# A two-layer SSD and HGRN2 encoder step: the norms' sums of squares as two fp32r passes, and one norm placed earlier in pieces

## The chip, the cores and the metric

The kernel runs on one core of a Trainium2 chip. The engines are TensorE (PE, with its weight loads as PEld), VectorE (DVE), ScalarE (ACT), GpSimd (POOL) and SyncE (SP, which issues the DMAs). The metric is the device time of one execution in microseconds (us), as a median over runs. [...]

## The reference

A trunk of two layers takes one step for a prompt of 1024 frames and for a running stream of 32 frames, with the same weights and a model width of 1024. Cut to what matters here:

```python
def rmsnorm(x, w):
    y = x * rsqrt(mean(x * x, axis=-1) + 1e-6)
    return y * w

for layer in (0, 1):
    h = rmsnorm(x, norm_w)
    x = x + (ssd_mixer if layer == 0 else hgrn_mixer)(h, ...)
    x = x + swiglu(rmsnorm(x, ffn_norm_w), w_gate, w_up, w_down)
y = rmsnorm(x, final_norm_w)
```

Inside the SSD mixer each of 4 groups of 512 channels is normed by its own mean square, and inside the HGRN mixer each of 8 heads of 128 channels:

```python
yg = yg * rsqrt(mean(yg * yg, axis=-1) + 1e-6)                 # SSD, per group
o  = o  * rsqrt(mean(o * o,  axis=-1) + 1e-6) * gnorm_w        # HGRN, per head
```

The outputs are the two sequences and the recurrent states and convolution rows of both streams.

## The kernel before

**Layout.** Channels lie on the 128 partitions, frames on the free axis. The frames are worked in two halves: the first has 512 frames of the prompt, the second the other 512 and the 32 of the running stream, 544 in all. [...] The residual stream `acc[h][m]` (8 tiles of 128 channels for each half) stays in SBUF.

**Products.** To keep fp32 accuracy with fp32r matmuls, each operand is split into a high part (an ACT copy to fp32r) and a low part (a DVE subtraction, L273 and L274 in `split`), and `product` adds three passes: high by high (L303), high by low (L304), low by high (L305). Weights are split in the same way after each load (L292, L293). The FFNs save multiplications with a Strassen-like scheme (`ffn_unit`, its three passes at L940 to L942).

**Norms.** `rstd_of` squares its tiles on ACT (L312), adds them on DVE into one tile `tot` (L316), and sums over the partitions with one fp32 matmul for each block against a 128x128 tile of ones (L320). ACT then takes Ln with scale and bias (L321) and Exp of -0.5 times that (L322). It is called for 4 SSD gates and 8 HGRN gates in each half, for `x_stat` (the statistics alone, kept in a tile that the caller names), and from `norm`, which goes on to scale and split all 8 tiles in one go (L353, L357, L358). `norm` is wrapped so that the scheduler takes its instructions 600 steps earlier than their place in the program (`HP`, `lifted`). `norm_pieces` (L860) does the scaling and splitting as 8 tasks for each block, without that lift, so that a caller can lay them among other tasks.

**Tiles.** The tag "n" has 4 buffers (`BUFS`), used for the squares, `rstd`, the scaled tile `xf`, the HGRN layer's decay factors, and two evacuation tiles of each FFN unit. The normed and split residual of the first half lies in the fixed tiles `XN`; that of the HGRN layer's second half takes 12 buffers of "x" and 4 of "cb" (`XN2`). In the HGRN layer the recurrent states use `st[0]` and `st[1]`; `st[2]` and `st[3]` are free.

**Order.** The framework's scheduler lays out each engine's instructions when the program is built, by program order, priority and when it expects operands to be ready; on the chip each engine takes its instructions in that order. The HGRN layer runs 16 units, heads 0 to 7 of the first half, then of the second. While the chunks of one head's recurrence run, a list of tasks is dealt out among them: the gate projection of this head, the output product of the last pair of heads (every second head), and the projections f, q and v of the next head. A gate (`hgrn_gate`) with its `rstd_of` ends each head. Before the change, head 6 of the first half has `norm(1, C_HGN, xns[1], XN2)` as its last task (L827); the projections of the second half's head 0, in head 7's list, are the first to read it. The input of that norm, `acc[1]`, is complete before the HGRN layer begins.

Of the kernel before, what the change touches and what calls it, by code (L numbers as in the profile page):

```python
# [9 lines left out]
F32R = mybir.dt.float32r  # L10
U32 = mybir.dt.uint32
AF = mybir.ActivationFunctionType
# [4 lines left out]
P = 128  # L17
# [5 lines left out]
LEN = (H1, SEQ - H1 + NS)  # L23
# [14 lines left out]
C_SSDN, C_CB, C_FFN, C_HGN, C_GN, C_HG, C_LB = 0, 8, 32, 48, 56, 72, 73  # L38
# [10 lines left out]
def trunk_kernel(ctx, tc, x_prompt, x_sample, state_ssd, cache_conv, state_hgrn,  # L49
# [5 lines left out]
    V, A, G, PE = nc.vector, nc.scalar, nc.gpsimd, nc.tensor  # L55

    cp = ctx.enter_context(tc.tile_pool(name="cp", bufs=1))
# [8 lines left out]
    def nm(s):  # L66
        uid[0] += 1
        return f"{s}_{uid[0]}"

    def T(tag, s, dt=F32):  # L70
        return tp.tile([P, WIDTH[tag]], dt, tag=tag, bufs=BUFS[tag], name=nm(s))

    def slot(tag, s):
        return T(tag, s, F32R) if isinstance(tag, str) else tag
# [19 lines left out]
    def psum_sc():  # L94
        return pm.tile([P, 512], F32, tag="sc", bufs=3, name=nm("sc"))

    def act(out, in_, f, **kw):
        A.activation(out=out, in_=in_, func=f, **kw)  # L98
# [32 lines left out]
    def place(w):  # L131
        used[0] += -(-w // 16) * 16
        return fixed[:, used[0] - -(-w // 16) * 16:][:, :w]
# [4 lines left out]
    make_identity(nc, ident)  # L138
    ones = place(P)
    V.memset(ones, 1.0)  # L140
    epsc = place(1)
    V.memset(epsc, EPS)
    lss = place(13)
# [127 lines left out]
    def split(xf, w, pair):  # L271
        xh, xl = pair
        act(xh[:, :w], xf, AF.Copy)  # L273
        tt(xl[:, :w], xf, xh[:, :w].bitcast(F32), SUB)  # L274
        return pair
# [31 lines left out]
    def rstd_of(tiles, blocks, scale, width, keep=None):  # L307

        tot = None
        for i, t in enumerate(tiles):  # L310
            sq = T("n", "sq")
            act(sq[:, :width], t, AF.Square)  # L312
            if tot is None:
                tot = sq
            else:
                tt(tot[:, :width], tot[:, :width], sq[:, :width], ADD)  # L316
        r = keep if keep is not None else T("n", "rstd")
        for (b0, bn) in blocks:
            ps = psum_sc()
            PE.matmul(ps[:, :bn], ones, tot[:, b0:b0 + bn], start=True, stop=True)  # L320
            act(r[:, b0:b0 + bn], ps[:, :bn], AF.Ln, bias=epsc[:, 0:1], scale=scale)  # L321
        act(r[:, :width], r[:, :width], AF.Exp, scale=-0.5)  # L322
        return r
# [3 lines left out]
    XN = [xnt[:, i] for i in range(16)]  # L327
    XN2 = ["x"] * 12 + ["cb"] * 4
# [15 lines left out]
    @lifted("norm")  # L344
    def norm(h, wc, out, tags, blocks=None, r=None):

        for (b0, bn) in blocks or ((0, LEN[h]),):
            mmb = BLK[h] if blocks is None else [(0, bn)]
            if r is None:
                r = rstd_of([acc[h][m][:, b0:b0 + bn] for m in range(KD)], mmb, 1.0 / D, bn)  # L350
            for m in range(KD):
                xf = T("n", "xf")
                stt(xf[:, :bn], acc[h][m][:, b0:b0 + bn], vc[:, wc + m:wc + m + 1], r[:, :bn], MUL, MUL)  # L353
                if m == len(out):
                    out.append((slot(tags[2 * m], "h"), slot(tags[2 * m + 1], "l")))
                xh, xl = out[m]
                act(xh[:, b0:b0 + bn], xf[:, :bn], AF.Copy)  # L357
                tt(xl[:, b0:b0 + bn], xf[:, :bn], xh[:, b0:b0 + bn].bitcast(F32), SUB)  # L358
        return out
# [8 lines left out]
    st = [place(TW) for _ in range(NG)]  # L368
# [442 lines left out]
    def hgrn_layer(after):  # L811
        units = [(h, e) for h in range(2) for e in range(8)]
        us = [{"S": None} for _ in units]
        for f in (hgrn_f, hgrn_q, hgrn_v):
            f(0, 0, us[0])
        for i, (h, e) in enumerate(units):
            u = us[i]
            tasks = [lambda: hgrn_g(h, e, u)]
            if e % 2 == 0 and i:
                ph, pe = units[i - 1]  # L820
                tasks += [lambda m4=m4: hgrn_out(ph, pe // 2, m4, [us[i - 2]["y"], us[i - 1]["y"]])
                          for m4 in range(2)]
            if i + 1 < len(units):
                nh, ne = units[i + 1]
                tasks += [lambda f=f: f(nh, ne, us[i + 1]) for f in (hgrn_f, hgrn_q, hgrn_v)]
            if (h, e) == (0, 6):
                tasks.append(lambda: norm(1, C_HGN, xns[1], XN2))  # L827
            if (h, e) == (1, 6):
                tasks += after[:1]
            if (h, e) == (1, 7):  # L830
                tasks += after[1:]
            u["o"] = T("ys", "ho")
            if e % 2 == 0:
                yt = sp.tile([P, 4 * TW], F32R, tag="Y", bufs=1, name=nm("hy"))[:, :4 * LEN[1]]
                yp = yt.rearrange("p (j t) -> p j t", j=4)
            u["yp"] = yp
            nch = len(CHUNKS[h])
            for c in range(nch):
                second = hgrn_chunk(h, e, c, u)
                q = -(-len(tasks) // (nch - c))  # L840
                for i2, t in enumerate(tasks[:q]):
                    if i2 == HB2:
                        second()
                    t()
                if q <= HB2:
                    second()
                tasks = tasks[q:]
            hgrn_gate(h, e, u)
        return [lambda m4=m4: hgrn_out(1, 3, m4, [us[-2]["y"], us[-1]["y"]]) for m4 in range(2)]
# [6 lines left out]
    def x_stat(h, keep):  # L856

        return rstd_of([acc[h][m][:, :LEN[h]] for m in range(KD)], BLK[h], 1.0 / D, LEN[h], keep)

    def norm_pieces(h, wc, out, blocks, r):  # L860

        def piece(m, b0, bn):
            xf = T("n", "xf")
            stt(xf[:, :bn], acc[h][m][:, b0:b0 + bn], vc[:, wc + m:wc + m + 1], r[:, b0:b0 + bn], MUL, MUL)
            if m == len(out):
                out.append((XN[2 * m], XN[2 * m + 1]))
            xh, xl = out[m]
            act(xh[:, b0:b0 + bn], xf[:, :bn], AF.Copy)
            tt(xl[:, b0:b0 + bn], xf[:, :bn], xh[:, b0:b0 + bn].bitcast(F32), SUB)
        return [lambda m=m, b=b: piece(m, *b) for b in blocks for m in range(KD)]  # L870
# [209 lines left out]
    def mixed(a, b):  # L1080

        out, k = [], 0
        for i, x in enumerate(a):
            out.append(x)
            while k < len(b) and k * len(a) < (i + 1) * len(b):
                out.append(b[k])
                k += 1
        return out + b[k:]
# [98 lines left out]
    xns, dts = [[], []], [None, None]  # L1187
# [12 lines left out]
    due, r = mixer_ffn(lambda after: ssd_layer(after, w0), 0, C_FFN, True)  # L1200
    for s, dst in ((0, conv_p), (1, conv_s)):
        ps = psum_sc()
# [7 lines left out]
    due, r = mixer_ffn(hgrn_layer, 1, C_FFN + 8, False)  # L1210
# [41 lines left out]
```

## Time and profile before

| What | us |
|---|---|
| median of 3 runs | 2893.22 |
| lowest and highest | 2892.77 and 2895.23 |
| the profiled execution's own time | 2895.71 |
| its span in the profile | 2894.0 |
| PE busy | 2843.8 |
| DVE busy | 2158.1 |
| ACT busy | 1563.9 |
| HGRN layer, roughly | 1600 to 2200 of the span |

The profile shows one execution. The time of an execution is that of the span and 1.7 us around it. In a timeline row the first number is the start from the span's start, the second the time covered, then engine, line, operation, tiles (out<-in), shape and how many instructions are merged in the row; in brackets stands how long the engine stood idle before it and what released it. Since L98, L101 and L104 are helpers that record every ACT, DVE tensor and DVE scalar-tensor operation, one reads those by the names of their tiles. The ends of matmuls are modelled, so their pace is read from one start to the next.

### The profile page before, as it was taken

Reading aid. Unit: us, or ns where it says so; the run is one execution under the profiler, and the core shown is the slowest. Engines: PE = TensorE matmul, PEld = TensorE weight load, DVE = VectorE, ACT = ScalarE, POOL = GpSimd, SP = SyncE. Lnnn points to the kernel's source line nnn. Section 1 sums busy time; section 2 is a strip of 40 time slices with the busy share of each in tenths; the row PEclk is TensorE's granted clock in tenths of the full one; section 3 lists DMA queues with packets and bytes.
Section 4 is the critical chain, followed back from the end, with each engine's and each line's share of the span. In section 5 each row is a group of like instructions: output and inputs, shape, how many; then the busy total and the mean of one; then the engine's idle time right before and its main releaser. Section 6 shows DMA issues by size and latency. Waiting matters only on the chain. (4 is left out here: it accounts for less than half of the span.)

```text
span 2894.0 us, 49037 instructions
## 1 busy us (share of the span) xinstructions
PE 2843.8 (98%) x19655; PEld 2615.4 (90%) x19655; DVE 2158.1 (75%) x3787; ACT 1563.9 (54%) x2951; POOL 43.2 (1%) x156
## 2 busy tenths in 40 slices
PE   7999999999999999999999999999999999999998
PEld 6777888999988999999999888899988999999998
DVE  6877797777787877887777555755568877887777
ACT  6755555564643644455444655755564644554445
POOL 0000000000000000000000000000000000000000
PEclk9999999999999999999999999999999999999999
DMA  5443434444332333323333222222222332333223
GB/s 159 121 108 111 107 79 126 113 111 108 106 90 88 106 106 95 110 81 101 97 96 114 79 75 73 60 77 74 79 78 92 113 95 91 118 96 95 88 88 112
DMA packets 401343, 283.39 MB, mean 98 GB/s; under 512 B 28873, under 2 KB 386778, under 8 KB 401114
## 3 DMA queue, kind: packets, MB, share of 16 engines
q1 hardware_dynamic: 401114, 280.25, 33.3%
q8 instruction: 154, 2.52, 0.4%
q14 instruction: 75, 0.61, 0.1%
HBM read 272.39 MB, written 7.82 MB: 97 GB/s over the span
## 5 line engine op out<-in xcount | busy, mean ns | idle before, releaser
L98 ACT ACTIVATE wh<-raw 128x512 fp32r<-128x512 f32 (+1 forms) x688 | 557.1, 818 | 556.8 <-PE mm L304 431.3
L303 PE MATMUL mm<-xn,wh 128*128 128x272 f32 (+2 forms) x1552 | 524.2, 338 | 1.7 <-ACT xn L98 1.3
L304 PE MATMUL mm<-xn,wh 128*128 128x272 f32 (+2 forms) x1552 | 519.0, 335 | 1.2 <-DVE xn L101 1.2
L305 PE MATMUL mm<-xn,wl 128*128 128x272 f32 (+2 forms) x1552 | 518.0, 334 | 1.2 <-DVE wl L101 1.2
L101 DVE TENSOR_TENSOR wl<-raw,wh 128x1024 fp32r<-128x1024 f32 x308 | 375.5, 1221 | 75.4 <-ACT wh L98 57.4
L101 DVE TENSOR_TENSOR fixed<-mm,fixed 128x272 f32<-128x272 f32 (+1 forms) x512 | 262.5, 523 | 194.4 <-PE mm L305 192.8
L304 PE MATMUL mm<-fl,wh 128*128 128x272 f32 (+1 forms) x1056 | 342.3, 324 | 0.9 <-DVE fl L101 0.8
L303 PE MATMUL mm<-fh,wh 128*128 128x272 f32 (+1 forms) x1056 | 341.4, 325 | 0.6 <-DVE fixed L101 0.6
L305 PE MATMUL mm<-fh,wl 128*128 128x272 f32 (+1 forms) x1056 | 341.7, 324 | 0.0
L303 PEld LDWEIGHTS mm<-xn,wh 128*128 128x128 f32 x1552 | 292.9, 189 | 32.1 <-issue 2.8
L305 PEld LDWEIGHTS mm<-xn,wl 128*128 128x128 f32 x1552 | 292.9, 189 | 31.1 <-issue 2.0
L304 PEld LDWEIGHTS mm<-xn,wh 128*128 128x128 f32 x1552 | 292.5, 188 | 29.3 <-DVE xn L101 1.7
L101 DVE TENSOR_TENSOR wh<-raw,wh 128x512 fp32r<-128x512 f32 x380 | 256.8, 686 | 43.5 <-ACT wh L98 40.9
L940 PE MATMUL mm<-th,wh 128*128 128x272 f32 (+1 forms) x912 | 260.2, 285 | 0.1
L942 PE MATMUL mm<-th,wh 128*128 128x272 f32 (+1 forms) x912 | 259.6, 285 | 0.2 <-DVE wh L101 0.2
L941 PE MATMUL mm<-tl,wh 128*128 128x272 f32 (+1 forms) x912 | 259.6, 285 | 0.0
L304 PEld LDWEIGHTS mm<-fl,wh 128*128 128x128 f32 x1056 | 198.7, 188 | 17.2 <-DVE fl L101 2.4
L303 PEld LDWEIGHTS mm<-fh,wh 128*128 128x128 f32 x1056 | 198.3, 188 | 16.6 <-DVE fixed L101 1.0
L305 PEld LDWEIGHTS mm<-fh,wl 128*128 128x128 f32 x1056 | 198.6, 188 | 15.3
L940 PEld LDWEIGHTS mm<-th,wh 128*128 128x128 f32 x912 | 171.6, 188 | 2.0 <-ACT s L98 1.4
L941 PE MATMUL sc<-xn,wh 128*128 128x272 f32 (+1 forms) x608 | 173.1, 285 | 0.0
L942 PE MATMUL sc<-xn,wh 128*128 128x272 f32 (+1 forms) x608 | 172.8, 284 | 0.0
(247 smaller groups left out, 6628.9 us busy)
## 6 DMA issues: line engine op xcount, KB each, us to landing
raw<-in_ffn_w_down_dram SPq DMA_DIRECT2D x90, 512.0 KB, 3.5
raw<-in_ffn_w_gate_dram SPq DMA_DIRECT2D x88, 512.0 KB, 3.9
raw<-in_ffn_w_up_dram SPq DMA_DIRECT2D x88, 512.0 KB, 4.8
raw<-in_ssd_in_w_dram SPq DMA_DIRECT2D x80, 512.0 KB, 4.2
raw<-in_hgrn_in_w_dram SPq DMA_DIRECT2D x64, 512.0 KB, 4.3
cumB<-cumd SPq DMA_DIRECT2D x64, 256.0 KB, 5.0
raw<-in_ssd_out_w_dram SPq DMA_DIRECT2D x32, 512.0 KB, 3.6
raw<-in_hgrn_out_w_dram SPq DMA_DIRECT2D x16, 512.0 KB, 3.3
```

Source lines behind the costliest of these rows:

```text
L98: A.activation(out=out, in_=in_, func=f, **kw)
L101: (eng or V).tensor_tensor(out=out, in0=a, in1=b, op=op)
L303: PE.matmul(ps[:, :bn], a, mh, start=(k == 0), stop=False)
L304: PE.matmul(ps[:, :bn], a, ml, start=False, stop=False)
L305: PE.matmul(ps[:, :bn], b, mh, start=False, stop=(k == n - 1))
L940: PE.matmul(ps[:, :n], a, mh, start=(k == 0 and not more), stop=False, skip_group_check=True)
L941: PE.matmul(ps[:, :n], a, ml, start=False, stop=False, skip_group_check=True)
L942: PE.matmul(ps[:, :n], b, mh, start=False, stop=(k == 3), skip_group_check=True)
```

## The change

There are two parts. First, `rstd_of` splits `tot` into a high and a low fp32r tile (`th`, `tl`, both of tag "n") and adds two fp32r passes against an fp32r copy of the ones in PSUM, where one fp32 matmul stood. Second, in the HGRN layer the second half's norm is taken apart: the statistics become the last task of head 5 (`x_stat`, kept in `st[2]`), and the scaling and splitting become eight pieces (one block of all 544 frames) laid evenly among head 6's tasks. `norm_pieces` gets an argument for the tiles it writes.

```diff
     ones = place(P)
     V.memset(ones, 1.0)
+    onesr = cp.tile([P, P], F32R, name="onesr")
+    A.activation(out=onesr, in_=ones, func=AF.Copy)
...
         r = keep if keep is not None else T("n", "rstd")
+        th, tl = split(tot[:, :width], width, (T("n", "th", F32R), T("n", "tl", F32R)))
         for (b0, bn) in blocks:
             ps = psum_sc()
-            PE.matmul(ps[:, :bn], ones, tot[:, b0:b0 + bn], start=True, stop=True)
+            PE.matmul(ps[:, :bn], onesr, th[:, b0:b0 + bn], start=True, stop=False)
+            PE.matmul(ps[:, :bn], onesr, tl[:, b0:b0 + bn], start=False, stop=True)
             act(r[:, b0:b0 + bn], ps[:, :bn], AF.Ln, bias=epsc[:, 0:1], scale=scale)
...
     def hgrn_layer(after):
         units = [(h, e) for h in range(2) for e in range(8)]
         us = [{"S": None} for _ in units]
+        r = []
...
+            if (h, e) == (0, 5):
+                tasks.append(lambda: r.append(x_stat(1, st[2])))
             if (h, e) == (0, 6):
-                tasks.append(lambda: norm(1, C_HGN, xns[1], XN2))
+                tasks = mixed(tasks, norm_pieces(1, C_HGN, xns[1], ((0, LEN[1]),), r[0], XN2))
...
-    def norm_pieces(h, wc, out, blocks, r):
+    def norm_pieces(h, wc, out, blocks, r, tags=XN):
...
             if m == len(out):
-                out.append((XN[2 * m], XN[2 * m + 1]))
+                out.append((slot(tags[2 * m], "h"), slot(tags[2 * m + 1], "l")))
```

`mixed` (L1080) lays the second list evenly among the first, so head 6's list becomes: gate projection, two pieces, output product, a piece, output product, a piece, f, two pieces, q, a piece, v, a piece.

## The prediction

> **What bounds the kernel now.** I read the page first, then the waits of PE, then windows around the largest wait, then the timeline there, and last the groups of instructions for the price of one.
>
> ```profile
> span 2894.0 us, 49037 instructions
> PE 2843.8 (98%) x19655; PEld 2615.4 (90%) x19655; DVE 2158.1 (75%) x3787; ACT 1563.9 (54%) x2951; POOL 43.2 (1%) x156
> ```
>
> PE is busy 98% of the span, but a matmul's end is modelled, so the pace has to come from starts. The timeline gives it (first and last row of a run of equal matmuls, and a sum of squares with the instruction behind it):
>
> ```profile
> 1898.03 0.29 PE L303 MATMUL mm<-h,wh 128*128 128x272 f32 x1
> ...
> 1900.91 0.28 PE L305 MATMUL mm<-h,wl 128*128 128x272 f32 x1
> ...
> 1817.78 0.39 PE L303 MATMUL mm<-xn,wh 128*128 128x512 f32 x1
> ...
> 1825.87 0.40 PE L305 MATMUL mm<-xn,wl 128*128 128x512 f32 x1
> ...
> 1903.76 1.08 PE L320 MATMUL sc<-sq,fixed 128*128 128x272 f32 x4
> 1904.68 0.38 PE L757 MATMUL sc<-hq,hk 128*128 128x128 f32 x2
> ...
> 1785.69 1.02 PE L320 MATMUL sc<-sq,fixed 128*128 128x512 f32 x2
> 1786.55 0.38 PE L757 MATMUL sc<-hq,hk 128*128 128x128 f32 x2
> ```
>
> The first pair is 24 matmuls, so 23 steps in 2.88 us: 0.125 us for an fp32r pass over 272 columns. The second is 36, 35 steps in 8.09 us: 0.231 us for 512 columns. They start without a pause, so PE is the bound by pace too. The plain fp32 product of L320 shows as two records for each block. In a second half (two blocks, x4) it holds PE for 1904.68 - 1903.76 = 0.92 us; in a first half (one block, x2) for 1786.55 - 1785.69 = 0.86 us.
>
> The waits of PE, and the windows of the one that matters here:
>
> ```profile
> PE mm L303 <- ACT h L98: 3.2, 1, 3.2
> PE sc L320 <- DVE sq L101: 2.7, 3, 1.7
> ```
> ```profile
> 960.00:985.00 25.00, 23.27 (x147) 20.79 (x147) 21.48 (x37) 16.36 (x30) 0.00 (x0) 1.00 0.24 79
> 1600.00:1826.00 226.00, 226.00 (x1097) 185.19 (x1095) 127.09 (x234) 129.90 (x204) 0.00 (x0) 1.00 0.26 73
> 1829.80:1833.00 3.20, 0.05 (x2) 0.02 (x1) 1.55 (x3) 2.82 (x5) 0.00 (x0) 1.00 0.21 79
> 1833.00:1834.80 1.80, 1.11 (x5) 0.72 (x5) 1.80 (x4) 1.80 (x3) 0.00 (x0) 1.00 0.00 0
> 1834.80:1838.30 3.50, 3.38 (x15) 3.38 (x16) 3.50 (x6) 0.83 (x2) 0.00 (x0) 0.51 0.33 94
> 1838.30:1842.00 3.70, 3.70 (x31) 3.70 (x31) 3.70 (x7) 1.96 (x4) 0.00 (x0) 1.00 0.14 53
> 1842.00:2130.00 288.00, 287.44 (x2216) 278.25 (x2215) 168.39 (x378) 167.19 (x295) 0.00 (x0) 1.00 0.27 76
> ```
>
> Columns are length, then busy time and count of PE, PEld, DVE, ACT, POOL, then granted clock, DMA share and GB/s. At 1829.8 PE stands still for 3.2 us, limps for 1.8 us, and then runs 3.5 us at a granted clock of 0.51: 15 matmuls, where the next window has 31 in 3.70 us. [...]
>
> The chain behind that pause, from the timeline:
>
> ```profile
> 1826.59 1.18 PE L320 MATMUL sc<-sq,fixed 128*128 128x272 f32 x4 [0.32 <-DVE sq L101]
> ...
> 1829.47 1.28 ACT L98 ACT_TABLE_LOAD   x1
> 1830.76 0.66 ACT L98 ACTIVATE rstd<-rstd 128x544 f32<-128x544 f32 x1
> ...
> 1831.45 2.18 DVE L104 SCALAR_TENSOR_TENSOR xf<-fixed,rstd 128x544 f32<-128x544 f32 x3 [2.81 <-ACT rstd L98]
> ...
> 1832.27 0.66 ACT L98 ACTIVATE h<-xf 128x544 fp32r<-128x544 f32 x1 [0.37 <-DVE xf L104]
> ...
> 1832.98 0.76 PE L303 MATMUL mm<-h,wh 128*128 128x272 f32 x4 [3.15 <-ACT h L98]
> ```
>
> This is the HGRN layer's norm of the second half: sums, Ln, Exp, scale and split in a row, with the first second-half projection waiting at the end.
>
> **The change part by part.** *1. The fp32 passes.*
>
> ```profile
> L320 PE MATMUL sc<-sq,fixed x90: 390/393/697, 133.6 to 2270.4; 128*128 128x272 f32 x60, 128*128 128x512 f32 x30
> ```
>
> The code calls `rstd_of` 15 times in each half (4 SSD gates, 8 HGRN gates, 3 norms or statistics): 15 x 2 records of 512 and 15 x 2 blocks x 2 records of 272, which is this row. The new product is two fp32r passes for each block, the same kind as L303. First half: 0.86 - 2 x 0.231 = 0.40 us, times 15 is 6.0. Second half: 0.92 - 4 x 0.125 = 0.42 us, times 15 is 6.3. Together **-12.3 us** of PE. [...]
>
> *2. The split in front of it.* Every call gains one ACT copy to fp32r and one DVE subtraction. The same two on a tile of the same size:
>
> ```profile
> L98 ACT ACTIVATE th<-xt 128x544 fp32r<-128x544 f32 x16 | 10.4, 653 | 11.4 <-DVE xt L101 11.2
> L101 DVE TENSOR_TENSOR tl<-xt,th 128x544 fp32r<-128x544 f32 x16 | 11.5, 720 | 0.1
> ```
>
> That is 0.65 and 0.72 us, 30 times: 20 us on ACT (54% busy) and 22 us on DVE (75%), hidden as load; what can cost is the 1.37 us of latency. What waits behind it is queued on PE, which takes matmuls in the planned order, and on ACT, where the Ln stands behind the copy. A typical HGRN gate, and the consumer of its result:
>
> ```profile
> 1934.09 0.66 ACT L98 ACTIVATE sq<-ho 128x544 f32<-128x544 f32 x1
> 1934.77 1.28 ACT L98 ACT_TABLE_LOAD   x1
> 1934.80 1.18 PE L320 MATMUL sc<-sq,fixed 128*128 128x272 f32 x4
> 1936.06 0.49 ACT L98 ACTIVATE rstd<-sc,fixed 128x272 f32<-128x272 f32 x1
> ...
> 1942.80 0.65 PE L303 MATMUL mm<-hy,wh 128*128 128x272 f32 x3
> 1943.09 0.72 DVE L101 TENSOR_TENSOR hy<-ho,hy 128x544 fp32r<-128x544 f32 x1
> ...
> 1944.41 0.29 PE L304 MATMUL mm<-hy,wh 128*128 128x272 f32 x1
> ```
>
> The table load for Ln already takes 1.28 us between Square and Ln. With the split it starts one copy later and covers the subtraction and the shorter passes, so Ln moves by about 0.65 us, not 1.37. An even head's result is wanted only with the next head's; an odd head's is read the moment it is there (1942.80). Five accumulators let PE do 15 matmuls (1.9 us) of the even head's share first, so of the 0.65 us I charge 0.3 us in each of the three pairs of the second half: **+1.0 us**. In the first half the same 15 matmuls are 3.5 us long and cover it. Bounds: 0, and 7 pairs at the full 1.37 us, 9.6 us. SSD gates have the next group's six convolutions between them and their consumer; cost nothing, and 1.37 us each if that cover were gone (then up to 11 us for eight).
>
> *3. Two statistics inside the FFNs*, where DVE is full (21.48 of 25 us in the window 960:985 above) and PE already stands at L320:
>
> ```profile
> 974.92 1.19 PE L320 MATMUL sc<-sq,fixed 128*128 128x272 f32 x4 [1.73 <-DVE sq L101]
> ...
> 2269.57 1.18 PE L320 MATMUL sc<-sq,fixed 128*128 128x272 f32 x4 [0.61 <-DVE sq L101]
> ```
>
> The split can add up to 1.37 us to each (+2.7), or the plan moves the product behind other matmuls and the wait itself goes (-2.3). I take 0.5 us each, **+1.0 us**. Four buffers of "n" hold the two evacuation tiles of a unit, the total, and now `th` and `tl`; `tl` may have to wait until the unit in flight has freed one, which is why I don't take zero.
>
> *4. The HGRN norm a head sooner.* Statistics go to the end of head 5's tasks, scaling and splitting become eight pieces among head 6's, and the first reader is head 7's task list. A head of the first half lasts some 27 us, from the sums of head 4's gate
>
> ```profile
> 1758.15 1.12 PE L320 MATMUL sc<-sq,fixed 128*128 128x512 f32 x2
> ```
>
> to those of head 5 at 1785.69; the chain takes 6.4 us (1826.59 to 1832.98). Its ACT and DVE work is the same as before and only moves; no DMA moves. So the pause goes with its slow clock: from 1829.8 to 1838.3 PE started 2 + 5 + 15 = 22 matmuls in 8.5 us, at 0.125 us each 2.75 us of work: **-5.7 us**. Late next are the weights of that projection, which were there already (the wait names `h` alone). Bounds: 0 and -5.7, with the 0.3 us at 1826.59 besides.
>
> *5.* The fp32r copy of `ones` is one 128-wide copy while the first loads are under way: nothing, at most the 0.65 us of the wider copy.
>
> Sum: -12.3 + 1.0 + 1.0 - 5.7 = -16.0 us. The profiled execution took 2895.71 us (span 2894.0), so it would take 2879.7; against the median of 2893.22, 2.5 us below it, **2877 us**.
>
> **The rivals.**
> *A, a wait takes the pause's place.* The statistics of the moved norm use "n" buffers just ahead of head 5's gate. Eight squares and seven sums in a row:
>
> ```profile
> L98 ACT ACTIVATE sq<-fixed 128x544 f32<-128x544 f32 x24 | 14.5, 650 | 0.0
> L101 DVE TENSOR_TENSOR sq<-sq,sq 128x544 f32<-128x544 f32 x33 | 23.8, 721 | 4.4 <-ACT sq L98 3.8
> ```
>
> 8 x 0.65 + 7 x 0.72 = 10.2 us; if the gate's buffers come only after them, the pair's output product is late by that less the 3.5 us of cover, 6.7 us, and the pause is paid back: 2893.2 - 12.3 + 2.0 - 5.7 + 6.7 = 2884. For it: gate and statistics share four buffers. Against: their input is finished long before, and DVE is 56% busy there (127.09 of 226).
> *B, PE isn't the bound.* [...] As a mechanism of this kernel: if a tenth of PE's time were slack, shorter passes would end in waits and only the pause would go: 2893.2 - 5.7 = 2887.5. Against: weight loads fill 278.25 of 288 us with 272 columns and 185.19 of 226 with 512, which is a load of 0.19 us against 0.231 us of matmul; the share follows the width, not slack. The same time, 2887 to 2890, comes out if the fp32r passes cost what L320 costs now, so that the change didn't do what it says.
> *C, slower.* PE takes its queue in order. If every sum of squares stood at its old place in that order, PE would wait for copy and subtraction, 1.37 us, at each of 30 calls: +41.1 - 12.3 - 5.7 = +23, 2916 us. It decides from 0.6 us a call on, (12.3 + 5.7) / 30. Against: today 30 calls stand 2.7 us for DVE in three waits, though the total is ready just ahead of many of them, so the order is laid out by when operands are due, and the split is laid out with it.
> *D, dearer latencies.* The waits of parts 2 and 3 near their upper bounds, +12.3 instead of +2: 2887.5.
>
> **How the numbers follow.** Forecast (2872 to 2881): 0.61. A: 0.13. D, shading up to 2887: 0.13. B or its like: 0.07. C: 0.06. The low end is -12.3 - 5.7 - 2.3 - 0.3 = -20.6, 2872; the high end takes in A and D up to their far ends, 2888. A measurement of this kernel can tell about 0.2%, 5.8 us, from no change: faster, below 2887.4, is the forecast, A and most of D, 0.86; within, 0.08; slower, C, 0.06.
>
> **What would show it.** Right: the L320 records become 0.125 and 0.231 us apart; no wait of L303 for `h` near 1830 and no window there at a clock of 0.51; copy and subtraction at 0.65 and 0.72 us, 30 each; the waits at the sum of squares stay within a few us in all. Wrong: a wait of PE for `tl` at many calls (C), a wait for `hy` after head 5 (A) or in each second-half pair (D), or PE's total lower by 12 us with the span unmoved (B).

## The result, and the profile after

| | before | after |
|---|---|---|
| median, us | 2893.47 (16 runs, 2890.63 to 2895.23) | 2900.14 (16 runs, 2897.48 to 2904.92) |
| ratio of after to before | | 1.0024, 95% interval 1.0016 to 1.0031 |
| profiled execution, us | 2895.71 | 2902.1 |
| its span, us | 2894.0 | 2900.4 |

The kernel became 0.24% slower; the forecast was 2877 us, 0.57% faster. Here is the head of the page of after:

```profile
span 2900.4 us, 49056 instructions
PE 2840.5 (98%) x19655; PEld 2616.5 (90%) x19655; DVE 2174.8 (75%) x3817; ACT 1578.5 (54%) x2982; POOL 58.5 (2%) x156
```

PE is busy 3.3 us less than before while the span is 6.4 us longer: the shorter passes are there, and PE stands still more. The waits of PE in after (engine, line, what was waited for: us in all, times, longest):

```profile
PE mm L307 <- DVE wl L101: 7.2, 4, 4.1
...
PE sc L776 <- ACT hkv L98: 3.8, 3, 1.9
PE mm L305 <- ACT xn L98: 3.7, 5, 2.1
...
PE sc L323 <- ACT th L98: 3.2, 4, 1.4
...
PE mm L305 <- ACT pre L98: 2.6, 1, 2.6
...
PE mm L306 <- DVE hy L101: 1.4, 2, 0.7
```

The 3.2 us for `h` that the prediction quoted is no longer in the list. In its place stand waits for the low part of weights (`wl`), for a tile of the normed residual (`xn`), a projection's evacuation (`pre`) and a chunk's state (`hkv`). Only the row for `th` names a tile that the change made. (Lines are four higher than before; L305 to L307 are the three passes of `product`, L323 and L324 the two passes of the sum, L776 was L772.)

Both traces have 19655 matmuls, so one can follow where the time went by subtracting the start of the n-th matmul before from the start of the n-th after. This table is worked out so from both traces:

| stretch of before, us | after falls behind by, us | what is there |
|---|---|---|
| 0 to 417 | -2.7 | start-up and passes |
| 417 to 470 | +3.3 | a 4.06 us wait for `wl`, then half clock |
| 470 to 740 | -0.8 | passes |
| 740 to 760 | +4.4 | waits for `wl` and `pre` |
| 760 to 1770 | -3.5 | passes; a half-clock stretch of before is missing |
| 1770 to 1820 | +7.9 | head 5's gate is late, then half clock |
| 1820 to 1860 | -6.4 | the pause of before is gone |
| 1860 to 2125 | -1.4 | passes, less what the pairs of heads lose |
| 2125 to 2160 | +3.7 | a wait for `xn`, then half clock |
| 2160 to the end | +1.9 | mostly a half-clock stretch at 2547 |

The sum is +6.4 us, the difference of the spans. The windows of after show the clock in these places (length, then busy time and count of PE, PEld, DVE, ACT, POOL, granted clock, DMA share, GB/s):

```profile
422.00:426.27 4.27, 0.21 (x2) 0.00 (x0) 4.15 (x10) 3.39 (x7) 0.74 (x2) 1.00 0.24 37
427.30:430.70 3.40, 3.40 (x17) 3.40 (x17) 3.33 (x5) 1.55 (x2) 0.35 (x1) 0.50 1.08 325
1799.50:1809.70 10.20, 8.66 (x24) 6.67 (x25) 6.50 (x12) 3.56 (x8) 0.00 (x0) 0.50 0.24 67
1829.00:1834.80 5.80, 5.80 (x27) 4.72 (x26) 5.15 (x9) 4.59 (x9) 0.00 (x0) 1.00 0.00 0
2137.40:2140.80 3.40, 3.40 (x10) 2.69 (x9) 3.40 (x6) 2.15 (x4) 0.00 (x0) 0.50 0.00 0
2547.00:2550.40 3.40, 3.40 (x17) 3.40 (x17) 3.26 (x6) 0.92 (x2) 0.00 (x0) 0.50 0.00 0
```

Where before paused (1829 to 1834.8), PE of after works without a break at full clock. But between 64 and 2870 us it runs 3.4 + 10.2 + 3.4 + 3.4 = 20.4 us at half clock; before had 6.8 (3.4 at 1834.8 and 3.4 at 1247.7). In such a stretch passes of 272 columns start 0.227 us apart (13 steps from 2547.09 to 2550.04), where 0.125 us is their step at full clock, so at most half of the 13.6 us more, 6.8 us, is time lost in this one execution. Each of the four starts in a wait of PE or within 1.7 us of the end of one (4.06, 1.94, 2.09 and 1.26 us long); that the wait brings it about is not shown. Three places have to be read closer.

**The wait at 422 us, in the SSD layer.** The timeline of after (start, duration, engine, line, operation, tiles; in brackets the idle time before it and its releaser):

```profile
420.87 1.27 DVE L401 TENSOR_TENSOR_SCAN dt<-fixed,dt 128x544 f32<-128x544 f32 x1
...
422.18 0.65 ACT L98 ACTIVATE dt<-dt 32x544 f32<-32x544 f32 x1 [5.16 <-DVE dt L401]
...
423.32 0.79 DVE L101 TENSOR_TENSOR dt<-dt 32x512 f32<-32x512 f32 x2
...
424.39 0.69 DVE L101 TENSOR_TENSOR yl<-Y,yh 128x512 fp32r<-128x512 f32 x1
...
425.00 1.22 DVE L101 TENSOR_TENSOR wl<-raw,wh 128x1024 fp32r<-128x1024 f32 x1
...
426.27 0.39 PE L307 MATMUL mm<-xn,wl 128*128 128x272 f32 x1 [4.06 <-DVE wl L101]
```

and the same three operations before:

```profile
423.37 1.27 DVE L397 TENSOR_TENSOR_SCAN dt<-fixed,dt 128x544 f32<-128x544 f32 x1
...
424.57 1.19 DVE L101 TENSOR_TENSOR wl<-raw,wh 128x1024 fp32r<-128x1024 f32 x1
...
425.82 0.40 PE L305 MATMUL mm<-xn,wl 128*128 128x272 f32 x1 [0.83 <-DVE wl L101]
```

Before, DVE made `wl` right behind the scan. In after it stands behind the rest of the `dt` chain and a `yl`, and ACT stands 5.16 us for the scan, with its other work behind the operation on `dt` that waits. DVE is not slower (1.22 us against 1.19); its order is another. No `th` and no `tl` is in these rows.

**The output product of a pair of heads.** After, second half, first pair:

```profile
1935.59 0.66 ACT L98 ACTIVATE sq<-ho 128x544 f32<-128x544 f32 x1
...
1936.28 0.66 ACT L98 ACTIVATE th<-sq 128x544 fp32r<-128x544 f32 x1
...
1938.25 0.49 ACT L98 ACTIVATE rstd<-sc,fixed 128x272 f32<-128x272 f32 x1
...
1941.00 0.65 ACT L98 ACTIVATE rstd<-rstd 128x544 f32<-128x544 f32 x1
...
1942.36 0.29 DVE L101 TENSOR_TENSOR fixed<-fixed,sc 128x128 f32<-128x128 f32 x1 [4.29 <-PE sc L776]
...
1942.53 0.37 PE L305 MATMUL mm<-hy,wh 128*128 128x272 f32 x1
...
1942.91 0.78 DVE L104 SCALAR_TENSOR_TENSOR ho<-ho,fixed,rstd 128x544 f32<-128x544 f32 x1
...
1944.71 0.66 ACT L98 ACTIVATE hy<-ho 128x544 fp32r<-128x544 f32 x1 [0.40 <-DVE ho L101]
...
1944.99 1.22 DVE L101 TENSOR_TENSOR wl<-raw,wh 128x1024 fp32r<-128x1024 f32 x1
...
1946.12 0.72 DVE L101 TENSOR_TENSOR hy<-ho,hy 128x544 fp32r<-128x544 f32 x1
```

and before, besides the rows that the prediction shows:

```profile
1939.45 0.65 ACT L98 ACTIVATE rstd<-rstd 128x544 f32<-128x544 f32 x1
...
1940.14 0.78 DVE L104 SCALAR_TENSOR_TENSOR ho<-ho,fixed,rstd 128x544 f32<-128x544 f32 x1
...
1941.94 1.23 DVE L101 TENSOR_TENSOR wl<-raw,wh 128x1024 fp32r<-128x1024 f32 x1
```

From Square to Ln it takes 1938.25 - 1935.59 = 2.66 us; before it took 1936.06 - 1934.09 = 1.97 (the prediction's rows): 0.69 us more, where 0.65 was expected. By the Exp this is made up: 1941.00 - 1935.59 = 5.41 us after Square, 1939.45 - 1934.09 = 5.36 before. But from Square to the low part of `hy` it takes 1946.12 - 1935.59 = 10.53 us against 1943.09 - 1934.09 = 9.00: 1.53 us more. The low part follows a `wl` in both. What is new is ahead of the scaling: before, DVE scales `ho` right behind the Exp (1940.14); after, it stands 4.29 us at an update of the recurrent state, which waits for PE and is laid out ahead of the scaling, and scales at 1942.91, though the Exp has ended at 1941.65. So here too it is DVE's order, and not the split's latency.

PE starts the product 1942.53 - 1935.59 = 6.94 us after Square, 7.28 before, and runs out of passes that do without the low part. From the first to the last start of its 96 passes it takes 14.25, 14.33 and 14.02 us in the three second-half pairs, 12.66, 12.64 and 12.66 before. Not all of that is lost: PE does 14 matmuls of the chunks in between, 4 before, and stands idle for at most 0.37 us. What is lost shows from one pair's first start to the next one's: 74.25 and 74.44 us in the second half, 74.64 and 74.67 before. Two heads should have saved 0.84 us there by their shorter passes, so a pair loses 0.4 to 0.6 us.

The first two pairs of the first half take 12.21 us, 11.32 before, with no other matmul more and 0.68 us idle; from start to start it is 66.06 us, 65.96 before, where 0.80 less was due. This loss of 0.9 us is not the split's, as `e3_passes_only` will show.

**Head 5's gate.** The moved statistics and the gate, in after:

```profile
1787.62 0.66 ACT L98 ACTIVATE th<-sq 128x544 fp32r<-128x544 f32 x1 [1.04 <-DVE sq L101]
...
1792.84 0.61 ACT L98 ACTIVATE sq<-ho 128x512 f32<-128x512 f32 x1
...
1796.38 0.48 PE L307 MATMUL mm<-hy,wl 128*128 128x512 f32 x1
...
1800.30 0.79 PE L776 MATMUL sc<-hkv 128*128 128x128 f32 x2 [1.94 <-ACT hkv L98]
...
1804.64 0.69 DVE L101 TENSOR_TENSOR hy<-ho,hy 128x512 fp32r<-128x512 f32 x1
```

The statistics' copy waits on ACT for their last sum, their Ln and Exp follow, and head 5's Square starts only at 1792.84; the low part of its `hy` is made at 1804.64. PE began that output product at 1791.0 and had used up what it could do of it at 1796.38; the next pass of it starts at 1804.53. That is the place that rival A named. Between the Ln of the statistics at 1789.93 and the Square ACT has no idle time: it is ACT's queue that is full there, and no row shows a wait for a buffer.

### The profile page after: what moved, and what is told of

Same layout as the page of the kernel before. It is cut to its first block, busy times and chain, and to the rows that moved or that the text cites. A ratio compares the mean times of both kernels' runs of the same rounds, so it can differ in the third digit from the quotient of the medians.

```text
span 2900.4 us, 49056 instructions
## 1 busy us (share of the span) xinstructions
PE 2840.5 (98%) x19655; PEld 2616.5 (90%) x19655; DVE 2174.8 (75%) x3817; ACT 1578.5 (54%) x2982; POOL 58.5 (2%) x156
## 4 chain that ended last, share of the span: by engine, by line
PE 86%; DVE 7%; ACT 3%; DMA 2%; issue 1%; SPq 0%; POOL 0%; DVEq 0%; ACTq 0%; POOLq 0%
PE mm L305 18%; PE mm L307 18%; PE mm L306 18%; PE mm L949 5%; PE mm L947 5%; PE mm L948 5%; PE sc L949 3%; PE sc L947 3%; PE sc L948 3%; PE sc L548 1%; PE sc L537 1%; DVE fixed L101 1%; PE sc L534 1%; DVE wh L101 1%; DMA fixed<-in_ssd_D_dram 1%
## 5 line engine op out<-in xcount | busy, mean ns | idle before, releaser
L305 PE MATMUL mm<-xn,wh 128*128 128x272 f32 (+2 forms) x1552 | 523.5, 338 | 6.8 <-ACT xn L98 3.7
L307 PE MATMUL mm<-xn,wl 128*128 128x272 f32 (+2 forms) x1552 | 518.7, 335 | 5.8 <-DVE wl L101 5.8
L305 PE MATMUL mm<-fh,wh 128*128 128x272 f32 (+1 forms) x1056 | 341.4, 325 | 0.6 <-DVE fixed L101 0.6
L307 PE MATMUL mm<-fh,wl 128*128 128x272 f32 (+1 forms) x1056 | 341.4, 324 | 0.0
L305 PEld LDWEIGHTS mm<-xn,wh 128*128 128x128 f32 x1552 | 293.4, 189 | 36.7 <-ACT xn L98 4.8
L307 PEld LDWEIGHTS mm<-xn,wl 128*128 128x128 f32 x1552 | 293.7, 189 | 35.9 <-DVE wl L101 6.7
L305 PEld LDWEIGHTS mm<-fh,wh 128*128 128x128 f32 x1056 | 198.4, 188 | 16.6 <-DVE fixed L101 1.0
L307 PEld LDWEIGHTS mm<-fh,wl 128*128 128x128 f32 x1056 | 198.7, 188 | 15.2
```

The costliest lines, as they stand in the source:

```text
L305: PE.matmul(ps[:, :bn], a, mh, start=(k == 0), stop=False)
L307: PE.matmul(ps[:, :bn], b, mh, start=False, stop=(k == n - 1))
```

## The experiments

Three explanations stood against each other at first: the split's latency in front of the sum; the place of its copy in ACT's queue, with what stands behind it; and the new norm's statistics ahead of head 5's gate. A fourth came out of the runs: two more instructions in the queues, and shorter passes, change the order that the scheduler lays out.

### The two parts alone, and the passes without the split

`e1_split_only` has the split and the fp32r passes with the old norm; `e2_norm_only` has the norm in pieces with the old fp32 sum (its diff is the second half of the change). `e3_passes_only` keeps the old norm and makes two fp32r passes without a split: the squares are written as fp32r, and the same total is taken twice against ones of 0.5, so the low part of the sum is left out.

```diff
-            sq = T("n", "sq")
+            sq = T("n", "sq", F32R)
...
-            PE.matmul(ps[:, :bn], ones, tot[:, b0:b0 + bn], start=True, stop=True)
+            PE.matmul(ps[:, :bn], onesr, tot[:, b0:b0 + bn], start=True, stop=False)
+            PE.matmul(ps[:, :bn], onesr, tot[:, b0:b0 + bn], start=False, stop=True)
```

> The first part alone: split and two fp32r passes, the HGRN norm as before. Theory W (the shorter passes are worth about 10 us of PE, but the split in front of them makes ACT and DVE queues wait, which costs more than it saves): the lag on the kernel before grows at 422, 750 and 2133 to 2153 us as in the changed kernel, some 11 us of waits, so 2894 to 2898 us, and the pause near 1830 us is still there. Theory M (the moved norm alone did the harm): 2881 to 2885 us.

> The second part alone: fp32 sums as before, the statistics at the end of head 5 and the norm in pieces in head 6. Theory Q (the statistics stand ahead of head 5's gate in the ACT queue, so the pause near 1830 us is only moved to the output product of heads 4 and 5, near 1795): 2891 to 2895 us, a wait of PE for hkv or hy near 1800 us and a stretch at half clock there. Theory of the prediction (the pause simply goes): 2887 to 2888 us.

> Two fp32r passes without any split: the squares and their sum are written as fp32r, and the product is taken twice against ones of 0.5, so the low part of the sum is left out of the result. PE does the same passes as in the changed kernel, ACT and DVE do what they did before. Theory W: 2893.5 less 10 to 12 us, 2881 to 2884 us. Theory B (PE is not the bound, shorter passes end in waits): 2891 to 2894 us.

| against before, 2892.52 | median, us | ratio | 95% interval |
|---|---|---|---|
| e1_split_only | 2902.81 | 1.0033 | 1.0021 to 1.0046 |
| e2_norm_only | 2889.66 | 0.9990 | 0.9982 to 0.9999 |
| e3_passes_only | 2886.34 | 0.9977 | 0.9968 to 0.9986 |

The passes alone gain 6.2 us; with the split in front of them 10.3 us are lost. So the split costs 2902.81 - 2886.34 = 16.5 us with the old norm, and part 1 is what makes the kernel slower. `e1` came out above both of its ranges; `e2` and `e3` lie between theirs, so each of the two theories had a part of it. With the split, the old norm's pause grows too, as this row of `e1_split_only` shows (3.15 us before):

```profile
1836.31 1.27 PE L305 MATMUL mm<-h,wh 128*128 128x272 f32 x4 [6.04 <-ACT h L98]
```

`e3_passes_only` also settles what the pairs lose. In the second half they take 12.63, 12.66 and 12.59 us without a split, and 73.76 and 73.73 us from start to start: there the passes gain all that was due. In the first half the pairs take 12.41 us with no split at all, and 66.30 us from start to start, more than in after. PE waits for the high part of `hy` there, in the first pair of `e3`:

```profile
1653.77 0.73 PE L305 MATMUL mm<-hy,wh 128*128 128x512 f32 x2 [0.84 <-ACT hy L98]
```

So the first half's loss comes with the two short passes and the order laid out for them.

### The statistics one head sooner

`e4_stats_head4` is the kernel after the change with the statistics at the end of head 4's tasks instead of head 5's; the pieces stay in head 6.

```diff
-            if (h, e) == (0, 5):
+            if (h, e) == (0, 4):
```

> The changed kernel with the statistics one head earlier still, at the end of head 4, whose gate nobody reads for 25 us. Theory Q: the wait near 1800 us and its half clock go, and the pause near 1830 does not come back, so 6 to 8 us less than the changed kernel, 2892 to 2894 us. If the pieces in head 6 (their buffers, their place among the tasks) make the wait: 2899 to 2901 us.

It measured 2893.36 us, ratio 1.0003 (0.9994 to 1.0012), 6.8 us below after, and within the first of its two ranges. Head 4's result is wanted a head later, so nothing waits for its gate at once, and the loss at head 5 is gone; the waits at 422, 750 and 2130 us are still there. The later experiments build on this kernel.

### Where the split costs: engine, buffers, passes

`e5_dve_split` makes the high part on DVE, so that ACT's queue has no copy; `e8_own_ring` gives the two halves buffers of their own; `e6_passes_head4` is `e4` with the passes of `e3` (no split, the low part left out).

```diff
-        th, tl = split(tot[:, :width], width, (T("n", "th", F32R), T("n", "tl", F32R)))
+        th, tl = T("n", "th", F32R), T("n", "tl", F32R)
+        V.tensor_copy(th[:, :width], tot[:, :width])
+        tt(tl[:, :width], tot[:, :width], th[:, :width].bitcast(F32), SUB)
```

```diff
-        th, tl = split(tot[:, :width], width, (T("n", "th", F32R), T("n", "tl", F32R)))
+        th, tl = split(tot[:, :width], width, (T("t", "th", F32R), T("t", "tl", F32R)))
```

> As the run with the statistics at head 4 (2893.4 us), with the high part of the split copied by DVE too, so that ACT has nothing of it. Theory H (the copy stands in the ACT queue waiting for DVE's last sum, and weight copies and evacuations behind it are what PE waits for): the waits near 422, 750 and 2133 to 2153 us go, 2884 to 2888 us. Theory L (the split's latency alone does it, wherever it runs; DVE gets 30 copies more): 2892 to 2898 us with the waits as they were.

> Two fp32r passes without a split (squares and sum written as fp32r, the low part of the sum left out of the result) together with the norm in pieces and its statistics at head 4. If the two gains seen apart add up (6 us for the passes, some 7 to 9 us for the norm once its statistics are clear of head 5's gate): 2877 to 2881 us, the best so far. If the freed time goes into the pair's output product instead: 2884 to 2887 us.

> As the run with the statistics at head 4, with two buffers of their own for the two halves of the split, in place of two of the four of the tag n. If the shortage of n buffers makes the waits: 2885 to 2890 us and the waits near 422 and 750 us shorter. Theories H and L: 2892 to 2895 us.

| against before, 2891.71 | median, us | ratio | 95% interval |
|---|---|---|---|
| e5_dve_split | 2902.02 | 1.0036 | 1.0024 to 1.0049 |
| e6_passes_head4 | 2881.0 | 0.9964 | 0.9951 to 0.9976 |
| e8_own_ring | 2894.06 | 1.0008 | 1.0000 to 1.0017 |

Taking the copy off ACT makes it worse, above both ranges, so ACT's queue alone is not the cause; since DVE gets 30 copies more, it doesn't say what is. Own buffers change nothing: 2894.06 against 2893.36, with the waits at 422 and 750 us as they were. Without the split, passes and norm add up: 2881.0, 10.7 us below the kernel before. Against it the split of `e4` costs 2893.36 - 2881.0 = 12.4 us, less than the 16.5 with the old norm, whose pause it lengthened.

### Which calls pay

In four kernels the fp32 sum comes back for some calls by a flag, as here for the SSD gates:

```diff
-        r = rstd_of([Y[:, j, :L] for j in range(4)], BLK[h], 1.0 / (4 * 512), L)
+        r = rstd_of([Y[:, j, :L] for j in range(4)], BLK[h], 1.0 / (4 * 512), L, whole=True)
```

`e7_lifted_whole` does it for the two lifted norms, `e9_ssd_whole` for the 8 SSD gates, `e10_hgrn_whole` for the 16 HGRN gates; `e11_norm_head4` has no split in any call.

> As the run with the statistics at head 4, but the two norms ahead of the FFNs' first halves, which are taken 600 steps early, keep the fp32 sum without a split: 28 of 30 calls are split. Theory H puts the waits near 750 us and at 2133 to 2153 us on the copy in these two calls: 2886 to 2889 us. If the waits come from the gates' splits: 2893 to 2895 us.

> Built on e4_stats_head4 (2893.4): the 8 SSD gates alone go back to the one fp32 sum without a split; the other 22 calls keep the split and the two fp32r passes. If the split in the SSD gates is what moved the weights' split near 422 us behind the dt chain and delays the lifted norm near 750 us, the wait of PE for wl near 422 falls from 4.2 us to about 1.4 and the one for pre near 750 from 2.7 to at most 1, against 8 x 0.43 = 3.4 us of passes paid back: 2890 to 2892. Rival (these stalls come from the other calls or lie in the plan anyway): both stalls stay, and the fp32 sums cost 3.4 us more: about 2897.

> Built on e4_stats_head4 (2893.4): the 16 HGRN gates alone go back to the one fp32 sum without a split. If the split's latency in front of the pairs' output products is the main loss (1.5 us in each of three second-half pairs, 0.9 us in each of four first-half pairs, 8 us together), the products return to 12.7 and 11.3 us, and 16 x 0.41 = 6.6 us of passes is paid back: about 2892, with the pairs' times as in the kernel before. Rival (the main loss lies in the SSD layer and in the lifted norms): the pairs change little and the time rises by the passes: 2898 to 2900.

> No split anywhere, the fp32 sums of the kernel before, and only the norm in pieces with its statistics at the end of head 4's tasks. If the move from head 5 to head 4 is worth by itself what it was with the split (6.8 us) or what the passes showed (5.3 us against the old place), 2886 to 2887 against 2892 of the kernel before, with no wait of PE above 1.5 us between 1750 and 1840. Rival (the statistics collide wherever they are put, and the gain in e4 came from undoing a loss that only the split has): as e2_norm_only, 2889.7 or more.

| fp32 sum in | median, us | ratio to before (95% interval) | less `e4` (2893.36) | passes given back | so lost there by the change |
|---|---|---|---|---|---|
| 2 lifted norms (e7) | 2891.11 | 0.9997 (0.9988 to 1.0006) | -2.3 | 0.8 | 3.1 |
| 8 SSD gates (e9) | 2888.76 | 0.9986 (0.9977 to 0.9994) | -4.6 | 3.3 | 7.9 |
| 16 HGRN gates (e10) | 2894.98 | 1.0010 (1.0002 to 1.0019) | +1.6 | 6.6 | 5.0 |
| all (e11) | 2887.69 | 0.9984 (0.9975 to 0.9993) | -5.7 | 12.3 | 18.0 |

Passes given back are the prediction's 0.40 and 0.42 us a call, so the last column holds whatever kept the calls from that gain: the split, and the order laid out for the short passes. The two can be told apart for all calls together: without a split the passes gain 2887.69 - 2881.0 = 6.7 of the 12.3 us (`e6` against `e11`), and the split costs the 12.4 us above. `e7` and `e10` lie between their two ranges, `e9` 1.2 us below its better range and `e11` 0.7 us above its own. (`e4` and `e7` ran beside other runs of the kernel before than the rest, whose medians lay within 0.8 us of each other; the last digit of a difference is not to be leaned on.) The single steps add up: -2.3 - 4.6 + 1.6 = -5.3 against -5.7 for all, which leaves 0.4 us for the four statistics, or 2.0 with the 1.6 us of their passes. In `e9` the place at 422 us is as before, though the other 22 calls are split; so the stall there comes from the gates:

```profile
424.26 1.19 DVE L101 TENSOR_TENSOR wl<-raw,wh 128x1024 fp32r<-128x1024 f32 x1
...
425.50 0.40 PE L307 MATMUL mm<-xn,wl 128*128 128x272 f32 x1 [0.84 <-DVE wl L101]
```

The waits near 750 us are gone with it, which none of the rows there had suggested: the row of `th` with a wait of 1.81 us in ACT's queue at 751.93 belongs to a lifted norm, and that is still split in `e9`. In after the gate just ahead of it scales its output at 739.56 us, 737.24 before, which fits a delay handed on, but was not tried by itself. In `e10` the pairs are back at 12.7 and 11.3 us, and 422 and 750 us keep their waits. Of these three groups it is the lifted norms that make the wait for `xn` near 2130 us: in `e7` it is gone.

### A split that nothing reads

`e12_idle_split` keeps all copies and subtractions of `e4`, but sums the unsplit total in fp32, so PE and Ln wait for neither half.

```diff
-            PE.matmul(ps[:, :bn], onesr, th[:, b0:b0 + bn], start=True, stop=False)
-            PE.matmul(ps[:, :bn], onesr, tl[:, b0:b0 + bn], start=False, stop=True)
+            PE.matmul(ps[:, :bn], ones, tot[:, b0:b0 + bn], start=True, stop=True)
```

> As e4_stats_head4, with the copy and the subtraction still made in all 30 calls, but the sum is again one fp32 product of the unsplit total, so nothing reads the two halves. If the split costs by its latency ahead of the sum, nothing waits for it now: as e11_norm_head4, 2886 to 2888, and the waits near 422 and 750 us are those of the kernel before. If it costs by the load and by the order that two more instructions in the queues of ScalarE and VectorE bring about, the stalls stay and the shorter passes are lost: 2899 to 2904.

It measured 2895.87 us (ratio 1.0011, 1.0002 to 1.0020), 8.2 us above `e11_norm_head4`, between the two expectations. The timeline says why:

```profile
426.59 1.22 DVE L101 TENSOR_TENSOR wl<-raw,wh 128x1024 fp32r<-128x1024 f32 x1
...
427.86 0.59 PE L305 MATMUL mm<-xn,wl 128*128 128x272 f32 x1 [8.47 <-DVE wl L101]
```

The stall of 422 us is there, twice as long, though nothing waits for the split: at this place it costs by the order that it brings about, not by its latency. Near 750 us it is another matter, as the lag on the kernel before shows (worked out as in the table of stretches):

| stretch of before, us | `e3`: passes, no split | `e12`: split, unread | `e4`: both | `e9`: neither in the SSD gates |
|---|---|---|---|---|
| 417 to 470 | 0.04 | 7.84 | 4.30 | -0.05 |
| 740 to 760 | 1.91 | 0.81 | 4.44 | -0.06 |

Near 750 us an unread split costs little (though PE comes there 7 us later in `e12`, which may hide a wait), and the passes alone make almost half of the loss; the rest is seen only where the sum reads the split. The pairs of the HGRN layer take 12.66 and 11.3 us here, as before: there too the cost needs a reader, and its rows showed a new order. Between 2125 and 2160 us it is the same: -0.48 in `e12`, 3.64 in `e4`, 0.06 in `e7`. So an idle instruction can bring about a costly order, and so can a changed product; whether latency or order makes the losses near 750 and 2130 us is not shown.

### Split only where nobody waits

The last two ask whether in the HGRN layer only the odd heads pay, whose result the output product reads at once. Both keep the fp32 sum in the SSD gates and the lifted norms; `e14_all_heads` splits all HGRN gates, `e13_even_heads` the even ones.

```diff
-        r = rstd_of([ot[:, :L]], BLK[h], 1.0 / P, L)
+        r = rstd_of([ot[:, :L]], BLK[h], 1.0 / P, L, whole=(e % 2 == 1))
```

> Built on e4_stats_head4: split and fp32r passes only in the 8 gates of even HGRN heads and the 4 statistics of x_stat, 12 calls; the SSD gates, the lifted norms and the gates of odd heads keep the one fp32 sum. If a split costs nothing where the result is wanted a head later, and costs only where a pair's output product reads it at once, the pairs take 11.3 and 12.7 us as in the kernel before, and against e11_norm_head4 (2887.7) the 8 gates save 4 x 0.40 + 4 x 0.42 = 3.3 us and the x_stat calls about 1: 2883 to 2885. Rival (every split costs by its place in the queues): the saving is eaten, 2887 to 2890.

> Built on e4_stats_head4: split and fp32r passes in all 16 HGRN gates and in x_stat; the SSD gates and the lifted norms keep the one fp32 sum. If the costs of the groups of calls add, 2893.4 - 4.6 (SSD gates whole) - 2.3 (lifted norms whole) = 2886.5, with second-half pairs of 14.3 us; and above e13_even_heads by the pairs' losses (3 x 1.6 + 2 x 0.9 = 6.6 us) less the odd heads' passes (3.3 us), so by 3 us. If the odd heads are not what costs in the pairs, e13 has pairs of 14.3 us too and e14 is the faster by 3 us.

| against before, 2893.40 | median, us | ratio | 95% interval | first second-half pair, us |
|---|---|---|---|---|
| e13_even_heads | 2885.36 | 0.9973 | 0.9963 to 0.9984 | 12.74 |
| e14_all_heads | 2887.96 | 0.9981 | 0.9972 to 0.9990 | 14.30 |

The pairs and the order of the two came out as the first explanation has it; the difference is 2.6 us, where 3 was expected. That it came so near is in part luck, since the 3 us took the pairs' durations as losses. From start to start a pair of `e14` is 0.6 us longer than one of `e13` in the first half (65.87 against 65.26) and 0.1 us in the second (74.31 and 74.26 against 74.17 and 74.24); with the 0.4 us of passes that its odd head should save, a pair loses 1.0 and 0.5 us. `e13` is 0.4 us above its bracket and `e14` 1.5 us above its number. `e13_even_heads` computes the full sum everywhere and is the best such version found, 8.0 us faster than the kernel before and 14.8 below the kernel after the change. Its page and its window after the start:

```profile
span 2882.5 us, 49054 instructions
PE 2835.6 (98%) x19655; PEld 2610.2 (91%) x19655; DVE 2165.3 (75%) x3799; ACT 1568.5 (54%) x2964; POOL 43.0 (1%) x156
```
```profile
64.00:2868.00 2804.00, 2785.65 (x19313) 2564.89 (x19312) 2112.19 (x3656) 1521.92 (x2840) 38.63 (x142) 1.00 0.33 96
```

The granted clock is 1.00 over the 2804 us, as it is in after over 64 to 2870 us with 20.4 us at half clock in them, so a short stretch would not show in this figure. The mean over the span is 0.998, where before has 0.996 and after 0.994.

## Why the prediction was wrong, point by point

- *Part 1, the passes, -12.3 us.* The mechanism was right, the size too large. By the median step of each width and line, times their count, the sums fell from 26.6 to 16.3 us, by 10.3; added up step by step, from 24.8 to 17.8, by 7.0. The prediction took the two passes of a sum as standing in a row with the others, but the plan puts them apart:

```profile
1936.99 0.52 PE L323 MATMUL sc<-th,onesr 128*128 128x272 f32 x2
...
1937.35 0.38 PE L761 MATMUL sc<-hq,hk 128*128 128x128 f32 x2
...
1937.83 0.44 PE L324 MATMUL sc<-tl,onesr 128*128 128x272 f32 x2
...
1938.13 0.33 PE L765 MATMUL sc<-fixed,hk 128*128 128x128 f32 x1
```

  The first pair holds PE for 1937.35 - 1936.99 = 0.36 us and the second for 0.30, 0.66 us together where 4 x 0.125 = 0.50 was taken. As a change by itself the passes gave 6.2 us (`e3_passes_only`), because some of the room went into waits of its own order (1.9 us at 747 us, and 1.1 us against what was due between the first two pairs of the first half).
- *Part 2, the split, +1.0 us.* This is the step that failed: it counted the split as latency behind cover, and put at nothing what two more instructions a call do to the order of the queues. The split cost 16.5 us with the old norm (`e1` less `e3`) and 12.4 with the new one at head 4 (`e4` less `e6`). "SSD gates ... cost nothing" (their upper bound was 11 us): the 8 gates lost 7.9 us, at 422 and 750 us. At 422 us it is not the 1.37 us of latency that the bound counted but the order of DVE and ACT, since an unread split stalls PE there too; at 750 us almost half of the loss is the passes' and the rest is seen only with a reader. The pairs were charged 0.3 us in each of three; they lose 0.4 to 0.6 us, and not by the 0.65 us to Ln, which was right to 0.04 and is made up by the Exp, but by a state update on DVE ahead of the scaling. In the first half "the same 15 matmuls ... cover it" was wrong as well, 0.9 us, but this loss is there without the split. The two lifted norms, 3.1 us by `e7` less `e4`, had no term.
- *Part 3, the statistics in the FFNs, +1.0 us.* Not far off: the gap of PE ahead of the sum near 975 us is 1.6 us, 1.9 before. For all four statistics the table of calls leaves a loss of 2.0 us, or 0.4 net of their passes, and differences of medians don't settle so little.
- *Part 4, the norm a head sooner, -5.7 us.* The pause and its slow clock went as forecast: 6.4 us between 1820 and 1860, and the granted clock is 1.00 from 1809.7 to 2137.4. That a slow clock goes with its pause was the prediction's assumption, and no run shows it as a rule; what shows is that both are in the trace of before and neither is in that of after. But rival A, given 0.13, is what happened: the statistics hold up head 5's gate, 7.9 us between 1770 and 1820, where A's price was 6.7. Its place and about its size were right; its mechanism, buffers that gate and statistics share, was not tried by a run, and the rows show ACT's queue instead (1787.62 to 1792.84). A's time of 2884 was missed all the same, since it kept the split, parts 2 and 3, at 2.0 us. With the statistics at head 4 the norm gains: 6.8 us between after and `e4`, and 4.8 us by itself (`e11_norm_head4` against the 2892.46 of its before).
- *Rivals.* D, dearer latencies, was priced at 12.3 us and so not far in size, but it reckoned with latency, and where rows or runs show the cause it is order. B didn't happen as a whole: the passes do shorten the time, by 6.2 to 6.7 of the 12.3 us. Its tenth of slack is what the 90% of the PEld row leaves of the span; that this measures PE's slack is not shown. C, a wait for the split at every call, didn't either: L323 waits 3.2 us in four places. A and D were reckoned as alternatives; losses at the places of both came together, and neither included a new order, so the range ended at 2888.

What stays open is why the scheduler lays `wl` behind the `dt` chain as soon as the SSD gates have two more instructions. The order in the traces shows that it does, and taking them out (`e9`) or leaving them idle (`e12`) shows that they are the reason; which of its estimates tips over was not tried. Nor was it tried why it lays a state update ahead of the scaling in the second half's pairs, or what of latency and order makes the losses near 750 and 2130 us.

## What to carry to other kernels

In a kernel whose queues are laid out by a planner, an added instruction can have a price even where no one waits for it (8.2 us here for 30 idle splits, `e12` less `e11`), and the price can appear where none of its rows stands: reckon it by running the instruction idle, not by its latency alone. Make an operation dearer in latency and cheaper on the bound engine only in those calls whose result is wanted late (here the even heads), and leave the others as they are. Count what a stretch loses from one start to the next of the same work, since the duration of a product also holds other work that moved into it. Work moved out of a pause must not be put in front of a result that someone reads at once; one head earlier made 6.8 us of difference.

## What was unexpected of the hardware

The granted clock fell to half after a wait of 1.25 us, and not each time. Before and after both have a wait for `wh` at about 1250 us (it ends at 1247.00 in before and at 1250.67 in after), 1.25 and 1.26 us in the row and 1.4 us from start to start beyond a matmul's own step of 0.125 us; before's is followed by a half-clock stretch and after's is not, and at 2540 us it is the other way round. The wait in before, then windows of after, then of before:

```profile
1247.00 0.39 PE L942 MATMUL mm<-xn,wh 128*128 128x272 f32 x1 [1.25 <-DVE wh L101]
```

```profile
1245.00:1252.00 7.00, 5.44 (x41) 5.00 (x40) 6.98 (x18) 1.32 (x2) 0.00 (x0) 1.00 0.01 2
```
```profile
2540.00:2547.00 7.00, 5.75 (x46) 5.53 (x45) 6.71 (x14) 3.24 (x7) 0.00 (x0) 1.00 0.00 0
1247.70:1251.20 3.50, 3.50 (x18) 3.50 (x17) 3.11 (x5) 1.03 (x2) 0.00 (x0) 0.51 0.00 0
```

The half-clock stretches last 3.4, 6.8 or 10.2 us at a granted clock of 0.50 or 0.51, and their length does not follow that of the wait: 3.4 us from 427.3 us on in after, 1.0 us behind the end of a wait of 4.06 us; 6.8 us at the same place in `e4` (426.3 to 433.2, its wait 4.0 us); 10.2 us in `e12` (422.7 to 432.9), from within the wait of 8.47 us on; and 10.2 us from 1799.5 us on in after, from within a wait of 1.94 us on. After the 2.56 us for `pre`, which end at 756.06 us in after, the clock is 1.00 (756.06 to 760). In these two traces a wait of 1.4 us was followed by 3.4 us at half clock, up to 1.7 us lost, in one execution and by nothing in the other; what decides it is not shown.
